# A masked softmax of a batched matmul: from scheduled tiles to hand-written engine programs with loops

## The chip, the cores and the metric

The kernel runs on one core of one Trainium2 chip. The metric is the device time of one execution in microseconds (us), lower is better. A core has five engines that run their own instruction streams: TensorE (PE in the profile; PEld is its weight load), VectorE (DVE), ScalarE (ACT), GpSimd (POOL) and SyncE (SP), and 16 DMA engines that move data. Most executions agree within some 0.3%, a few are over 1.5% longer.

## The reference

```python
# x: 16 x 512 x 512, weight: 512 x 512, scale = 0.125, mask = strict lower triangle, all f32
y = scale * np.matmul(x, weight)
y = np.where(mask == 1, y, -1e9)
y_exp = np.exp(y - np.max(y, axis=-1, keepdims=True))
out = y_exp / np.sum(y_exp, axis=-1, keepdims=True)      # f32
```

16.8 MB of x are read and 16.8 MB are written, with 1 MB of weights. Row r has r unmasked columns, so the upper half of each matrix needs only the first 256 columns.

## The kernel before

The work is cut into 16 units of 1 MiB. A *unit* takes, for two matrices of the batch, the upper (even unit) or lower (odd unit) 256 rows, laid on 128 partitions as 4 row groups. Two units are a *pair*. A unit goes through: load (SP queue), cast to bf16 (VectorE), 16 transposes (TensorE), their eviction from PSUM (where TensorE puts its results) half by VectorE and half by ScalarE, 16 products and 4 additions of the mask's band (TensorE), 4 exponentials with row sums (ScalarE), reciprocals and 4 scalings (VectorE), store (SP queue). Tiles come from pools, and the framework puts in the semaphores.

```python
def multiply(u):
    NC = (u % 2 + 1) * HB                                # 256 columns, or 512
    for t in range(T):
        py = psum_y.tile([P, N], FP32, name="py")
        for kt in range(KT):
            seq(nc.tensor.matmul(py[:, :NC], lhsT=xt[:, kt, t], rhs=w_bf[:, kt, :NC], ...))
        seq(nc.tensor.matmul(py[:, h * HB : NC], lhsT=ident_bf, rhs=band[:, h, t], ...))
        seq(nc.scalar.activation(out=ot[:, t, :NC], in_=py[:, :NC], func=AF.Exp, ...,
                                 accum_out=rsum[:, t : t + 1]))

def normalise(u):
    seq(nc.vector.reciprocal(rinv, st_sum.pop(u)))
    for t in range(T):
        seq(nc.vector.tensor_scalar_mul(ot[:, t, :NC], ot[:, t, :NC], rinv[:, t : t + 1]))
    ...
# [...] loads in the order x0, m0, weights, m1, x1, m2, x2, m3, x3 ... (m: a 64 KB block of the mask)
for u in range(U + 1):                                   # all written out, 16 units
    if u + 1 < U: transpose(u + 1)
    # [...] cast(u + 2), evict(u + 1)
    if u < U: multiply(u)
    if u >= 1:
        normalise(u - 1); store(u - 1)
        if u - 1 + X_BUFS < U: load(u - 1 + X_BUFS)
```

Loads and stores share the one SP queue; there are 8 load buffers and 8 store buffers.

The softmax here doesn't subtract the row's maximum and nothing guards it: scores larger than these inputs give would overflow.

## Time and profile before

| | before |
|---|---|
| time, median of 3 (range) | 90.67 us (90.64 to 90.68) |
| profiled execution: time, span | 90.53, 88.75 us |
| first load issued, first packet | 0.74, 2.18 us |
| last store issued | 80.01 us |
| its 16 parts landed: median, last | 86.19, 87.73 us |
| last instruction | 88.75 us |

The span runs from the first to the last instruction of the profiled execution; the rest of the measured time, 1.78 us, lies outside it. The page cuts the span in 40 slices of 2.2 us, where a 9 means busy for 90% or more. The prediction below shows the page's own lines. TensorE is full but stops 11 us before the end (at 77.3 us; VectorE at 80.0), and the DMA is full from slice 3 to the end. Each of the 37 transfers leaves 16 landing records (592 in all), one for the share of each DMA engine, and what follows waits for the last: the last store's come from 85.71 to 87.73 us and the last instruction at 88.75, so the end is that of the *slowest* of 16.

### The profile page before, as it was taken

To read this page: it belongs to the slowest core of one execution; us is meant where nothing else is said; L and a number is where in the kernel's file an instruction comes from. 1 tells how busy PE (TensorE), PEld (TensorE's weight loads), DVE (VectorE), ACT (ScalarE), POOL (GpSimd) and SP (SyncE) were. 2 spreads that over 40 slices of the span, in tenths; PEclk is the share of its full clock that TensorE was granted. 3 is DMA by queue.
4 is the path that set the end of the run, shared out by engine and by line. 5 is a ranking of instruction groups with operands and counts; after the bars stand their busy time and mean duration, and the time that the engine had idled before them with its cause. 6 is when DMAs were issued, how large, how long until landed. Compare 5 with 4: busy or idle time off the path is not lost.

```text
span 88.8 us, 1632 instructions
## 1 busy us (share of the span) xinstructions
PE 71.3 (80%) x596; PEld 49.3 (56%) x596; DVE 60.6 (68%) x124; ACT 55.2 (62%) x154; POOL 7.3 (8%) x20
## 2 busy tenths in 40 slices
PE   4984409999999999999999999999999999800000
PEld 1324109875795598479659857965895695300000
DVE  5866485479799779949986987976594998070000
ACT  5401461887797686969777787977778786710000
POOL 7620000002001000200010020002000202000000
PEclk9999655899999999999999999999999999997555
DMA  0899999999999999999999999999999999999970
GB/s 15 306 373 384 381 376 428 417 432 428 414 425 417 425 436 428 402 417 432 428 428 417 428 421 421 425 436 425 421 417 432 425 421 425 428 432 428 425 306 26
DMA packets 5334, 34.95 MB, mean 394 GB/s; under 512 B 592, under 2 KB 1104, under 8 KB 1104
## 3 DMA queue, kind: packets, MB, share of 16 engines
q1 hardware_dynamic: 5328, 34.87, 94.6%
q8 instruction: 4, 0.07, 0.3%
q14 instruction: 2, 0.02, 0.0%
HBM read 18.09 MB, written 16.78 MB: 393 GB/s over the span
## 4 chain that ended last, share of the span: by engine, by line
PE 72%; DMA 10%; DVE 3%; SPq 2%; ACT 1%; DVEq 0%; issue 0%; ACTq 0%
PE py L116 47%; PE pt L92 16%; DMA xf<-in_x_dram 10%; PE py L125 8%; DVE ot L152 1%; DVE xb L83 1%; SPq L163 1%; SPq L78 1%; ACT ot L135 1%; PE py L215 0%; SPq L167 0%; DVEq L284 0%; DVE rinv L150 0%; ACTq L284 0%
## 5 line engine op out<-in xcount | busy, mean ns | idle before, releaser
L116 PE MATMUL py<-w_bf,xt 128*128 128x256 bf16 (+1 forms) x256 | 50.0, 329 | 0.0
L135 ACT ACTIVATE ot<-py 128x256 f32<-128x256 f32 (+1 forms) x64 | 31.2, 493 | 7.5 <-PE py L125 7.1
L116 PEld LDWEIGHTS <-xt 128*128 128x128 bf16 x256 | 24.8, 99 | 12.2
L103 ACT COPY xt<-pt 128x1024 bf16<-128x1024 bf16 x16 | 16.2, 1012 | 12.9 <-PE pt L92 8.8
L152 DVE TENSOR_SCALAR ot<-ot,rinv 128x256 f32<-128x256 f32 (+1 forms) x64 | 23.5, 431 | 0.8
L83 DVE CAST xb<-xf 128x2048 bf16<-128x2048 f32 x16 | 19.5, 1220 | 5.0 <-DMA xf<-in_x_dram 5.0
L92 PE MATMUL pt<-ident_bf,xb 128*128 128x128 bf16 x256 | 17.8, 225 | 3.7 <-DVE xb L83 3.7
L92 PEld LDWEIGHTS <-xb 128*128 128x128 bf16 x256 | 16.6, 115 | 5.8 <-DVE xb L83 4.9
L125 PE MATMUL py<-band,ident_bf 128*128 128x256 bf16 x64 | 17.6, 275 | 0.0
L102 DVE COPY xt<-pt 128x1024 bf16<-128x1024 bf16 x16 | 11.0, 687 | 6.2 <-PE pt L92 6.2
L135 ACT ACTIVATION_READ_ACCUMULATOR ot<-py 128x1 f32 x64 | 12.8, 200 | 0.0
L154 POOL MEMSET ot<- 2x256 f32 x8 | 3.6, 448 | 65.7 <-DVE ot L152 65.7
L125 PEld LDWEIGHTS <-ident_bf 128*128 128x128 bf16 x64 | 6.3, 99 | 4.2
L180 PE MATMUL py<-zeros 128*128 128x512 bf16 x12 | 5.2, 619 | 1.2 <-DVE zeros L177 1.2
L150 DVE RECIPROCAL rinv<-rsum 128x4 f32<-128x4 f32 x16 | 2.7, 168 | 2.8 <-ACT ot L135 2.8
L186 DVE MEMSET ot<- 128x1024 f32 x4 | 3.6, 912 | 0.6 <-issue 0.6
L180 PEld LDWEIGHTS <-zeros 128*128 128x128 bf16 x12 | 1.6, 144 | 3.9 <-issue 2.8
L226 DVE CAST band<-py 64x256 bf16<-64x256 f32 x4 | 1.6, 414 | 2.5 <-PE py L215 2.5
L215 PE MATMUL py<-diag_bf,spread 128*128 128x256 bf16 x8 | 1.6, 339 | 1.2 <-DVE diag_bf L202 1.2
L226 ACT CAST band<-py 64x256 bf16<-64x256 f32 x4 | 1.4, 367 | 1.4 <-DVE band L226 1.4
L193 ACT ACT_TABLE_LOAD x1 | 1.3, 1283 | 0.7 <-PEq L270 0.7
L215 PEld LDWEIGHTS <-spread 128*128 128x128 bf16 x8 | 0.9, 111 | 1.5 <-issue 1.3
(14 smaller groups left out, 7.5 us busy)
## 6 DMA issues: line engine op xcount, KB each, us to landing
xf<-in_x_dram SPq DMA_DIRECT2D x16, 1024.0 KB, 13.7
out_dram<-ot SPq DMA_DIRECT2D x16, 1024.0 KB, 11.9
w_f<-in_weight_dram SPq DMA_DIRECT2D x1, 1024.0 KB, 7.0
diag_f<-in_mask_dram SPq DMA_DIRECT2D x4, 64.0 KB, 7.7
```

The costliest lines, as they stand in the source:

```text
L83: seq(nc.vector.tensor_copy(xb, st_x.pop(u)))
L92: nc.tensor.transpose(st_pt[u][kt // 2][:, kt % 2, t], xb[:, t].rearrange("p (k kt) -> p kt k", kt=KT)[:, kt], ident_bf,)
L102: seq(nc.vector.tensor_copy(xt[:, 0:2], pt[0]))
L103: seq(nc.scalar.copy(xt[:, 2:4], pt[1]))
L116: nc.tensor.matmul(py[:, :NC], lhsT=xt[:, kt, t], rhs=w_bf[:, kt, :NC], start=(kt == 0), stop=(kt == KT - 1),)
L125: nc.tensor.matmul(py[:, h * HB : NC], lhsT=ident_bf, rhs=band[:, h, t], start=False, stop=True, skip_group_check=True,)
L135: nc.scalar.activation(out=ot[:, t, :NC], in_=py[:, :NC], func=AF.Exp, bias=0.0, scale=float(scale), accum_out=rsum[:, t : t + 1],)
L152: seq(nc.vector.tensor_scalar_mul(ot[:, t, :NC], ot[:, t, :NC], rinv[:, t : t + 1]))
L154: seq(nc.gpsimd.memset(ot[0:2, 0, :HB], 1.0 / N))
L180: seq(nc.tensor.matmul(idle, lhsT=zeros[:, :P], rhs=zeros, start=True, stop=True))
L186: nc.vector.memset(ots[i][:, :, HB:], 0.0)
L226: seq(copy(band[half, h, t : t + 2, g * P : (g + 1) * P], src[half, :, g]))
```

## The change

Its intent is to take instruction fetches, waits and VectorE instructions away. Everything stands in one section with hand-made semaphores. TensorE's program is a loop over 8 pairs that starts on a 256-instruction edge, ScalarE's is a loop of two rounds over 4 pairs, and VectorE's is written out; both start on a 128-instruction edge. A pair does both transposes, then both products. One `tensor_tensor` with a broadcast operand normalises a unit. The second load and the second mask block go ahead of the weights.

```diff
-    const = ctx.enter_context(tc.tile_pool(name="const", bufs=1))
-    [...] all pools
+    section.enter_context(tc.tile_critical(no_gpsimd_drain=True))
+    [...] fixed buffers and 59 semaphores
     load(0)
     load_mask(0)
-    seq(nc.sync.dma_start(w_f32, weight...))
-    load_mask(1)
-    load(1)
+    load(1)
+    load_mask(1)
+    nc.sync.dma_start(w_f32, weight...).then_inc(s_w, 16)
     [...]
-        for t in range(T):
-            seq(nc.vector.tensor_scalar_mul(ot[:, t, :NC], ot[:, t, :NC], rinv[:, t : t + 1]))
+        nc.vector.tensor_tensor(
+            out=ot, in0=ot, in1=r.unsqueeze(2).to_broadcast([P, T, NC]), op=ALU.mult
+        ).then_inc(s_norm, 1)
     [...]
+    tensor.addr_align(BLOCK, max_nops=0)
+    [...]
+    with tensor.Fori(1, U // 2 + 1) as n:
+        for i in range(2):
+            tensor.wait_ge(s_cast[i], n)
+            transpose(i)
+        with tensor.If(n < 2):
+            spin(3)
+            [...] spread the mask into the band
+        multiply(0, n)
+        multiply(1, n)
+    section.close()
+    with tc.tile_critical(no_gpsimd_drain=True):
+        nc.sync.wait_ge(s_end, 16 * OUT_BUFS)
+        nc.sync.sem_clear(s_end)
```

## The prediction

> **What bounds the kernel now.** I read the page's busy slices first, then its DMA queues, then the waits of the sync engine's queue, then the groups by form, then windows over the last microseconds, and last the trace's single DMA packet and landing records.
>
> ```profile
> PE   4984409999999999999999999999999999800000
> DVE  5866485479799779949986987976594998070000
> DMA  0899999999999999999999999999999999999970
> GB/s 15 306 373 384 381 376 428 417 432 428 414 425 417 425 436 428 402 417 432 428 428 417 428 421 421 425 436 425 421 417 432 425 421 425 428 432 428 425 306 26
> q1 hardware_dynamic: 5328, 34.87, 94.6%
> q8 instruction: 4, 0.07, 0.3%
> q14 instruction: 2, 0.02, 0.0%
> ```
>
> TensorE is full from slice 8, but it and every other engine stop by slice 36; the DMA is full from slice 3 to slice 38. At the middle rate of about 425 GB/s, 34.87 MB take 82.0 us. The first packet starts at 2.2 us, the first 13 us run at 376 to 384 GB/s, and the last data lands near 87.7 us. So the transfers set the end, though the page's chain of work is 72% TensorE.
>
> ```profile
> SPq L158 <- DVE ot L152: 49.8, 15, 9.6
> SPq L284 <- DMA out_dram<-ot: 7.1, 2, 4.7
> ...
> 80.01 0.54 SPq L158 DMA_DIRECT2D out_dram<-ot  x1
> ...
> 84.50:85.00 0.50, 0.00 (x0) 0.00 (x0) 0.00 (x0) 0.00 (x0) 0.00 (x0) 0.50 0.97 410
> 85.00:85.50 0.50, 0.00 (x0) 0.00 (x0) 0.00 (x0) 0.00 (x0) 0.00 (x0) 0.50 0.97 410
> 85.50:86.00 0.50, 0.00 (x0) 0.00 (x0) 0.00 (x0) 0.00 (x0) 0.00 (x0) 0.50 0.51 213
> 86.00:86.50 0.50, 0.00 (x0) 0.00 (x0) 0.00 (x0) 0.00 (x0) 0.00 (x0) 0.50 0.35 147
> 86.50:87.00 0.50, 0.00 (x0) 0.00 (x0) 0.00 (x0) 0.00 (x0) 0.00 (x0) 0.50 0.31 131
> ```
>
> The last store is issued at 80.01 us and the end waits for stores alone. The windows (next to last column: mean busy share of the 16 DMA engines) show a ragged end: full to 85.5, then about a third of the engines busy for 1.5 us more. The landing records say which: the 16 parts of the last store land between 85.71 and 86.46 for ten engines, and between 87.14 and 87.73 for six. Parts of one load land within 0.5 us of each other until 20 us; from 23.8 us one straggles by 1.2 us, later two, four, six. The packet records name a cause: four packets of 16,384 bytes on queue 8 (instructions) start at 21.5, 35.5, 50.4 and 63.3 us and take 0.9 to 1.1 us; two of 8,192 bytes on queue 14 come at 35.9 and 39.2. Six fetches, six late engines.
>
> [...]a pair of units has 146 TensorE instructions in 7.86 us, so 256 take 13.8 us, against 13 to 15 us between the fetches. [...]each of 16 engines signals its own share and only all 16 mean landed; the landing records show just that, so the slowest engine sets the end. [...]No tensor_tensor is in this trace[...].
>
> **The change part by part.** The groups by form that I calculate with:
>
> ```profile
> L116 PE MATMUL py<-w_bf,xt 128*128 128x512 bf16 x128 | 31.6, 379 | 0.0
> L83 DVE CAST xb<-xf 128x2048 bf16<-128x2048 f32 x16 | 19.5, 1220 | 5.0 <-DMA xf<-in_x_dram 5.0
> L103 ACT COPY xt<-pt 128x1024 bf16<-128x1024 bf16 x16 | 16.2, 1012 | 12.9 <-PE pt L92 8.8 <-ACT ot L135 4.1
> L152 DVE TENSOR_SCALAR ot<-ot,rinv 128x512 f32<-128x512 f32 x32 | 13.4, 483 | 0.3
> L102 DVE COPY xt<-pt 128x1024 bf16<-128x1024 bf16 x16 | 11.0, 687 | 6.2 <-PE pt L92 6.2
> L152 DVE TENSOR_SCALAR ot<-ot,rinv 128x256 f32<-128x256 f32 x32 | 10.1, 379 | 0.5
> ```
>
> *Instruction fetches.* The changed TensorE program is about 190 instructions in a loop that starts on a 256-instruction edge, so none of the four 16 KiB fetches should fall into the busy part; the ScalarE and VectorE programs start on 128-instruction edges and hold fewer than 128, so the two 8 KiB ones go too. What stays is at the start, before data flows. The end moves from the slowest of the late engines, 87.73, to the slowest of the others, 86.46: -1.27 us. This is on the path.
>
> *Transfers.* The same 33 transfers of 1 MiB and four mask blocks, one queue, same order but for one load ahead of the weights. Loads 3 to 7 no longer wait for earlier landings (4.0 us of waits), but DMA was never short of work there: 0.
>
> *Edges.* The section adds a barrier after the first one and one more hop at the end: some +0.25 us before the first load is issued (an estimate from the 0.4 to 0.5 us that one complete barrier takes at the end of this trace). At the end one wait replaces four semaphore waits in a row (0.25 us), which pays for the extra hop: 0.
>
> *Normalising.* Per pair, 4 x 317 + 4 x 420 ns (start to start in the timeline) = 2.95 us become [...]1.22 + 2.29 = 3.51 us: VectorE gains 0.56 us of work per pair. Its pair is then two evictions 1.3, a gap of 0.3 between them, two reciprocals with a self-wait 0.5, 3.5, two casts 2.4: 8.0 us. In the middle this is hidden. At the end the last unit's 2.29 against 1.68 is exposed to the last store's issue.
>
> *Order on TensorE.* Before, unit u+1's transposes run ahead of unit u's products, and a pair takes 7.86 us with no idle. Now a pair is two transposes (1.78), then two products (2.19 + 3.89). The first product needs both halves of its eviction: ScalarE is free about 0.72 us after the last matmul of the pair before and copies for 1.01, so TensorE starts at 1.8 to 1.9 in place of 1.78. [...]Pair: 7.86 + 0.1 to 0.3 = 8.0 to 8.15.
>
> *First pair.* Its products now wait for both transposes, the whole mask and the weights. Tile 1 lands at about 9.1 (where the weights landed), cast to 11.0, transposes at half clock to 12.9 (they took 1.90 cold before), eviction and mask to 13.9, three spins and four spreads to 15.3, copies to 16.3: products at 16.4 against 15.0. But two units are then ready: the first pair ends near 22.8, against 23.2.
>
> *Sum for compute.* 22.8 + 7 x 8.0 to 8.15 = 78.8 to 79.9; last exponential 0.7, reciprocal 0.3, product 2.3: the last store is issued at 82.1 to 83.2 in place of 80.0. The first load took 1.44 us from issue to first packet, and the last store's first packet ran at 83.59, so the store is in time if issued by 82.15 + 0.25 = 82.4. Overrun: 0 to 0.8 us, say 0.3.
>
> *Total.* 90.67 - 1.27 + 0.25 + 0.3 = about 90.0.
>
> **The rivals.** *(a) Compute takes the bound over.* The slack of the last store, 2.1 us, is nearly all spent. Every 0.1 us on a pair is worth 0.7 us at the end: a pair of 8.4 us would give 92, and a loop-back that fetches (0.9 to 1.1 us per fetch here) would give 97. For it: VectorE's pair at 8.0 has no room left. Against: the edge alignment is there just for this. *(b) The fetches are not what makes engines late,* or another comes near the end (leaving the loop): then the end stays ragged, and the change only adds its edges: 90.9 to 91.5. *(c) All hidden and the early dips shrink too:* the mask blocks cost short dips (141 to 200 GB/s for 0.2 us each); two of them now stand next to each other, the gain is at most 0.3: 89.2.
>
> **Range and chances.** My path is 90.0; (c) and an absent overrun give 89.2; a pair of 8.25 us gives 91.3. So 89.1 to 91.5. Faster by over 2% means under 88.86, below the transfers' floor as I have it: 6%. Slower by over 2% means over 92.48, a pair of over 8.4 us: 8%. Within 2%: 86%.
>
> **What would show it.** Right: no packet of 16,384 bytes on queue 8 between 3 and 80 us; the last store's 16 landings within 0.8 us; DMA share falling from 1.0 to 0 in half a microsecond; same GB/s in the middle; VectorE's product at 1.2 and 2.3 us; pair period 8.0 to 8.15; last store issued at 82 to 83. Wrong: fetches or long idle of TensorE at the loop's branch, a DMA share under 0.9 before the last store (compute is the bound), stragglers without fetches (rival b), or a first load issued later than 1.2 us.

The sum came to 90.67 - 1.27 + 0.25 + 0.3 = 89.95, "about 90.0". The 1.22 and 2.29 us of the products came from the cut rule, for no `tensor_tensor` had been measured; VectorE's pair of 8.0 us and, through the last store at 82.1 to 83.2, the overrun of 0.3 use them. That a loop on an edge has no fetches was an estimate: the 16 KB fetches of before start 12.9 to 14.9 us apart, and at 146 TensorE instructions in 7.86 us that is 239 to 278 of them, some 256 to a fetch and half as many to one of 8 KB.

## The result

| us | before | after |
|---|---|---|
| median of all runs | 90.68 (4 runs) | 91.56 (91.33 to 93.88, 4 runs) |
| ratio of fast runs, 95% interval | | 1.0084 (1.0064 to 1.0104) |

A ratio is the mean time of one kernel's fast runs over that of the other's fast runs of the same rounds, so it is not quite the ratio of the medians. The change made the kernel 0.8% slower: the same within 2%, but clearly not the hoped-for gain, and just above the range that was given.

The profiled run of that measurement fell in the slow state (93.88 us), so the unaltered kernel was run again. All four runs of it were fast (91.48 to 91.63, ratio 1.0099), and its profile, of a run of 91.48 us, is "after" from here on. This is its page: the busy slices of two engines, the clock that TensorE was granted, the DMA, and the DMA queues with their packets, MB and share.

```profile
span 89.4 us, 1673 instructions
...
PE   0995179699999999999999999999999999950000
DVE  2865727966089979997998899799889979719000
PEclk9999855699999999999999999999999999998555
DMA  0799999999999999999999999999999999999860
GB/s 15 286 348 351 393 370 425 429 425 425 433 425 418 422 433 425 425 425 433 422 425 429 425 429 433 425 422 425 433 422 425 433 429 418 425 436 418 359 271 7
q1 hardware_dynamic: 5328, 34.87, 93.9%
q8 instruction: 1, 0.02, 0.1%
q14 instruction: 2, 0.02, 0.1%
```

The bytes and the middle rate (some 425 GB/s) are those of before. The fetches have gone: queue 8 has one packet in place of four, and the packet records put the start of all three that are left between 1.9 and 2.2 us, before the first data packet at 2.46 (the 16 KB one lasts to 3.3). Yet the last slice of the DMA is as thin as before. The windows of the last microseconds show why (each line: the window, its length, busy time of the five engines, the clock, the mean share of the 16 DMA engines, GB/s):

```profile
86.00:86.50 0.50, 0.00 (x0) 0.00 (x0) 0.00 (x0) 0.00 (x0) 0.00 (x0) 0.50 0.68 279
86.50:87.00 0.50, 0.00 (x0) 0.00 (x0) 0.00 (x0) 0.00 (x0) 0.00 (x0) 0.50 0.08 33
87.00:87.50 0.50, 0.00 (x0) 0.00 (x0) 0.00 (x0) 0.00 (x0) 0.00 (x0) 0.50 0.04 16
87.50:88.00 0.50, 0.00 (x0) 0.00 (x0) 0.00 (x0) 0.00 (x0) 0.00 (x0) 0.50 0.04 16
88.00:88.50 0.50, 0.00 (x0) 0.00 (x0) 0.00 (x0) 0.00 (x0) 0.00 (x0) 0.50 0.00 0
```

Before, a third of the engines worked on for 1.5 us. Now the share drops to 0.04, and one engine of 16 is a share of 0.06: a *single* engine holds the end. The landing records of the last store say the same:

```
last store's parts landed (us)   median   last six                               last instruction
before                           86.19    87.14 87.18 87.22 87.52 87.65 87.73    88.75
after                            86.86    86.88 86.89 86.90 86.91 86.93 88.38    89.38
```

Six late engines have become one, and the one is as late against the median (1.52 us) as the latest of the six was (1.53). The lag of the last part behind the median, transfer by transfer, shows how it got there:

```
after: median landing   27.6   47.2   57.0   66.8   76.6   83.9   86.9
lag of the last part    0.48   0.48   0.83   1.22   1.80   2.01   1.52
lag of the next to last 0.31   0.45   0.45   0.45   0.45   0.50   0.07
```

No fetch happens in that time, but one engine drifts: it loses 1.5 us between 47 and 84 us and the second-latest loses nothing. The last store lets the others wait a little (their engines idle for about half a microsecond in front of it, for it was issued late), so 0.5 us of the lag is hidden again.

Where the time went, from the two profiled runs:

| us | before | after | difference |
|---|---|---|---|
| first load issued | 0.74 | 0.97 | +0.23 |
| moved by 15 us (packets under way counted in part) | 4.717 MB | 4.521 MB | |
| last store issued | 80.01 | 82.71 | +2.70 |
| last store landed, median engine | 86.19 | 86.86 | +0.67 |
| last store landed, last engine | 87.73 | 88.38 | +0.65 |
| last instruction after that | 1.02 | 1.00 | -0.02 |
| outside the span | 1.78 | 2.10 | +0.32 |
| sum | 90.53 | 91.48 | +0.95 |

0.20 MB fewer by 15 us are 0.46 us at 425 GB/s; 0.23 of it is the later first load. The first two issues of the sync engine, the after kernel's first and then the one of before (start, length, line):

```profile
0.97 0.67 SPq L121 DMA_DIRECT2D xf<-in_x_dram  x1
```

```profile
0.74 0.67 SPq L78 DMA_DIRECT2D xf<-in_x_dram  x1
```

The compute side did what was expected of it. Two groups by form of the after kernel, with count, busy time and mean ns:

```profile
L206 DVE TENSOR_TENSOR ot<-ot,rinv 128x2048 f32<-128x2048 f32 x8 | 18.3, 2292 | 0.3
L206 DVE TENSOR_TENSOR ot<-ot,rinv 128x1024 f32<-128x1024 f32 x8 | 9.8, 1224 | 0.3
```

From its timeline, two evictions of VectorE that stand one pair apart, and the sync engine's last store (start, length; in brackets the idle time before and what ended it):

```profile
40.55 0.69 DVE L197 COPY xt<-pt 128x1024 bf16<-128x1024 bf16 x1 [0.35 <-PE pt L302]
...
48.51 0.69 DVE L197 COPY xt<-pt 128x1024 bf16<-128x1024 bf16 x1 [0.35 <-PE pt L302]
...
82.71 0.54 SPq L140 DMA_DIRECT2D out_dram<-ot  x1
```

One instruction of 2.29 us replaces four of 483 ns, one of 1.22 replaces four of 379; the pair takes 48.51 - 40.55 = 7.96 us; the last store goes out at 82.71.

### The profile page after: what moved, and what is told of

The parts are those of the page before. It is cut to its first block, busy times and chain, and to the rows that moved or that the text cites. A ratio compares the mean times of both kernels' runs of the same rounds, so it can differ in the third digit from the quotient of the medians.

```text
span 91.8 us, 1665 instructions
## 1 busy us (share of the span) xinstructions
PE 74.4 (81%) x587; PEld 49.8 (54%) x595; DVE 65.8 (72%) x76; ACT 56.6 (62%) x154; POOL 6.2 (7%) x20
## 4 chain that ended last, share of the span: by engine, by line
PE 73%; DMA 7%; DVE 6%; SPq 3%; issue 2%; ACT 0%; ACTq 0%; DVEq 0%
PE py L317 47%; PE pt L302 16%; PE py L324 8%; DMA diag_f<-in_mask_dram 7%; DVE ot L206 2%; SPq L121 2%; DVE band L228 2%; PE py L336 1%; DVE xb L193 1%; SPq L125 1%; PE py L351 0%; DVE diag_bf L214 0%; ACT ot L285 0%; DVE rinv L204 0%; ACTq L267 0%
## 5 line engine op out<-in xcount | busy, mean ns | idle before, releaser
L317 PE MATMUL py<-w_bf,xt 128*128 128x256 bf16 (+1 forms) x248 | 49.3, 331 | 1.3 <-DVE band L228 0.8
L285 ACT ACTIVATE ot<-py 128x256 f32<-128x256 f32 (+1 forms) x64 | 31.4, 491 | 14.9 <-PE py L324 13.7
L317 PEld LDWEIGHTS py<-w_bf,xt 128*128 128x128 bf16 x256 | 25.1, 100 | 15.1 <-issue 1.7
L206 DVE TENSOR_TENSOR ot<-ot,rinv 128x1024 f32<-128x1024 f32 (+1 forms) x16 | 28.1, 1759 | 0.5
L302 PE MATMUL pt<-ident_bf,xb 128*128 128x128 bf16 x256 | 16.6, 225 | 3.7 <-DVE xb L193 3.7
L302 PEld LDWEIGHTS pt<-ident_bf,xb 128*128 128x128 bf16 x256 | 15.8, 115 | 5.6 <-DVE xb L193 4.7
L324 PEld LDWEIGHTS py<-band,ident_bf 128*128 128x128 bf16 x64 | 6.4, 100 | 4.3
L336 PE MATMUL py<-zeros 128*128 128x512 bf16 x15 | 6.8, 631 | 2.0 <-DVE zeros L231 2.0
L178 POOL MEMSET ot<- 2x256 f32 x8 | 2.4, 304 | 71.1 <-DVE ot L206 71.1
L336 PEld LDWEIGHTS py<-zeros 128*128 128x128 bf16 x15 | 2.1, 145 | 5.0 <-issue 5.0
L351 PE MATMUL py<-diag_bf,spread 128*128 128x512 bf16 x4 | 1.9, 633 | 0.0
```

The lines of the kernel that those rows point to most:

```text
L206: nc.vector.tensor_tensor(out=ot, in0=ot, in1=r.unsqueeze(2).to_broadcast([P, T, NC]), op=ALU.mult).then_inc(s_norm, 1)
L285: nc.scalar.activation(out=ots[b][:, t, :NC], in_=pys[t][:, :NC], func=AF.Exp, bias=0.0, scale=float(scale), accum_out=rsums[b][:, t : t + 1],
L302: last = tensor.transpose(pts[i][kt // 2][:, kt % 2, t], xb[:, t].rearrange("p (k kt) -> p kt k", kt=KT)[:, kt], ident_bf,)
L317: tensor.matmul(pys[t][:, :NC], lhsT=xts[h][:, kt, t], rhs=w_bf[:, kt, :NC], start=(kt == 0), stop=(kt == KT - 1),)
L324: tensor.matmul(pys[t][:, h * HB : NC], lhsT=ident_bf, rhs=band[:, h, t], start=False, stop=True, skip_group_check=True,).then_inc(s_py[h] ...
L336: tensor.matmul(pys[0], lhsT=zeros[:, :P], rhs=zeros, start=True, stop=True)
```

## The experiments

Four theories of the loss were on the table. *A, compute:* the later last store (normalising, a longer pair, the cold first pair) sets the end. *B, the slow engine:* one DMA engine drifts for another reason than the fetches and sets the end, so their removal gains nothing. *D, the start:* the new load order costs early bandwidth. *The edges:* what stands before the first load, after the last landing and outside the span. The expectations use these letters, and three more: *C* is B made precise (one engine loses about 2 us of its own between 28 and 80 us, in every kernel), *E* is the edges, and *F*, added last, is a reason for the drift. All runs gave right results. The ranges given for e_raw1, e_raw_best and e_flat hold one or two slow executions each, which the ratios leave out. The trace of e_order is of an execution of 93.72 us and that of e_raw_best of one of 91.40, 1.0 and 0.5 us above their medians.

**The unaltered kernel again** gave the profile above.

> The changed kernel once more, unaltered, for a profile in the fast state (the first one fell in the slow state, at 93.88 us). Theory A, compute has become the bound: about 91.5 us, pairs of 7.96 us on TensorE from 25.4 us on, last store issued at 84.5 to 84.7 us, and several DMA engines idle for about 1 us right before the last store's packets. Theory B, the transfers still bound it because some engines are delayed by fetches at the start or by something else: the engines' shares of the last store stay back to back with the store before, with no idle before them, and the landings are ragged by 1 us or more.

The median was 91.56, ratio 1.0099 (1.0082 to 1.0116). Fifteen engines had idle time before the last store and the sixteenth had nearly none: that is B's picture, not A's.

**A warm TensorE.** The granted clock is halved during the first pair (5 and 6 in slices 6 to 8; 0.50 from 11 to 16 us). With more idle matmuls it stayed up (in the page below; its mean is 0.967 in place of 0.921).

```diff
-WARM = 12
+WARM = 16
             transpose(i)
+            if i == 0:
+                with tensor.If(n < 2):
+                    spin(10)
```

> Four more idle matmuls at the start and ten between the first and the second unit's transposes, so that TensorE's clock does not fall before the first pair. Theory A: second transposes take 1.0 us in place of 1.9, spreads and first products run at full clock, the first pair ends near 22.5 us in place of 25.4, all later pairs come 2.5 to 3 us earlier, and the time falls to the transfers' floor, 89.3 to 90.0 us. Theory B: the pairs come earlier just the same, but the time changes by less than 0.3 us.

The page's clock row, the last store in the sync engine's timeline, and two windows of the end:

```profile
PEclk9999999999999999999999999999999999999655
```

```profile
81.38 0.54 SPq L140 DMA_DIRECT2D out_dram<-ot  x1
```

```profile
86.00:86.50 0.50, 0.00 (x0) 0.00 (x0) 0.00 (x0) 0.00 (x0) 0.00 (x0) 0.50 0.09 33
...
87.50:88.00 0.50, 0.00 (x0) 0.00 (x0) 0.00 (x0) 0.00 (x0) 0.00 (x0) 0.50 0.00 0
```

The clock is full and the last store goes out 1.33 us earlier (81.38 against 82.71). The fifteen engines end about 0.47 us earlier (median 86.39), the sixteenth only 0.18 (88.20). The time: 91.43, ratio 1.0086 (1.0069 to 1.0103). 1.33 us of compute bought 0.13 us, which is within the noise. A falls.

**Normalising of the last unit as before**, by four `tensor_scalar`.

```diff
+        if u == U - 1:
+            for t in range(T):
+                last = nc.vector.tensor_scalar_mul(ot[:, t], ot[:, t], r[:, t : t + 1])
+            last.then_inc(s_norm, 1)
+            return
```

> Only the last unit is normalised by four scalar products of 0.42 us (start to start) in place of one tensor product of 2.29 us; nothing else. Theory A: last store issued 0.6 us earlier, time lower by 0.5 to 0.6 us, about 90.9 us. Theory B: within 0.15 us of the changed kernel.

The last store went out at 82.04, 0.67 us earlier, and the time did not follow: 91.64, ratio 1.0117 (1.0084 to 1.015), last landing 88.64. A falls here too.

**No alignment.**

```diff
-    nc.vector.addr_align(BLOCK // 2, max_nops=0)
-    nc.scalar.addr_align(BLOCK // 2, max_nops=0)
-    tensor.addr_align(BLOCK, max_nops=0)
```

> The changed kernel without the three instructions that start the programs of TensorE, VectorE and ScalarE at a block's edge. If the edges matter, TensorE's loop now straddles one and fetches in the loop: instruction packets of 16,384 bytes in most pairs, 1 us or more of TensorE idle at each, 95 us or more. If loops fetch nothing[...], no packets after 25 us and the time within 0.3 us of the changed kernel, perhaps lower because the fetches at 2 us are gone.

91.45, ratio 1.0083 (1.0066 to 1.01). The three early fetches vanish, two of 8 KB come at 37.6 and 53.9 us, none of 16 KB at all, and TensorE shows no stall at the loop's branch (busy 54.22 of the 55 us from 25 to 80, against 54.42 with the alignment). The last landing was 88.62. The alignment buys nothing here: this loop of some 190 instructions ran its eight rounds without a 16 KB fetch where it happened to start. Why, no run shows.

**The fetches put back.** TensorE's loop was written out on top of the warm kernel. It is the direct test of the prediction's first term.

```diff
-    with tensor.Fori(1, U // 2 + 1) as n:
+    for n in range(1, U // 2 + 1):
 [...] e_warm's edit, and plain tests of n inside
```

> The kernel with the warm clock, TensorE's program written out in place of its loop, so that its instruction fetches fall into the transfers again. Theory C: one DMA engine loses about 2 us of its own between 28 and 80 us (packets of 320 to 360 ns in place of 309, all in one chain) in every kernel, and is last in all of them; fetches on other engines are then hidden: four packets of 16,384 bytes, time within 0.4 us of the 91.43 us of the looped one. My prediction's theory, fetches are on the path: 1.0 to 1.3 us slower, 92.5 us.

The page's instruction queue, and the windows of the end:

```profile
q8 instruction: 5, 0.08, 0.3%
```

```profile
86.50:87.00 0.50, 0.00 (x0) 0.00 (x0) 0.00 (x0) 0.00 (x0) 0.00 (x0) 0.50 0.27 115
87.00:87.50 0.50, 0.00 (x0) 0.00 (x0) 0.00 (x0) 0.00 (x0) 0.00 (x0) 0.50 0.31 131
87.50:88.00 0.50, 0.00 (x0) 0.00 (x0) 0.00 (x0) 0.00 (x0) 0.00 (x0) 0.50 0.12 49
```

```
last store's parts landed (us)   median   last six
e_warm (loop)                    86.39    86.47 86.51 86.55 86.60 86.84 88.20
e_warm_unroll (written out)      86.58    86.97 87.92 88.07 88.19 88.31 88.43
```

Four fetches of 16 KB come back (28.8, 39.6, 53.2, 68.8 us, 0.93 to 1.01 us each), and with them four more late engines and the third of a share in the windows. The time stays: 91.43, ratio 1.0084, against 91.43 and 1.0086 with the loop (other rounds, on another chip). So a fetch does make an engine late, as the prediction said, and that is hidden behind an engine that is late anyway, as it did not. How late, the packet records show: the fetch takes its 0.93 to 1.01 us, the data packet that starts as it ends takes 0.70 to 0.85 in place of 0.31, so some 1.3 to 1.5 us in all, and the five late engines land 1.34 to 1.85 us behind the median. In the kernel before, the four fetches took 0.89 to 1.10 us and the data packet behind each 0.77 to 0.86, some 1.43 to 1.56 us in all (0.63 and 0.95 with the two of 8 KB), and the engine stays late: the lag of the last part was 1.52 us at 22 us, after the first fetch, and 1.46 at 35.

**Less work for one engine.** If one engine is slow, a store that spares it should let it catch up. The store of unit 10 was split into 120 and 8 rows, in three kernels: on the warm one, on its written-out form and on the kernel before. I supposed that this spares the slow engine one store's share, 2.45 us (the measured time from store to store), if it is the last-numbered; no run shows which engine a row goes to, nor the slow engine's number.

```diff
+        if u in SPLIT:                                   # SPLIT = (10,)
+            nc.sync.dma_start(dst[:60], src[:120]).then_inc(done, 16)
+            nc.sync.dma_start(dst[60:], src[120:]).then_inc(done, 16)
+        [...] else as before; the final wait counts one transfer more
```

> The kernel with the warm clock; the store of unit 10 is issued as 120 rows and 8 rows[...]. Theory C, with the slow engine the last-numbered one: it ends 0.6 us before the others, [...]last landing near 87.0 in place of 88.2 us, time 90.2 to 90.6 us. If the slow engine is another, or the lag is not an engine's own: 91.4 to 92.0 us.

> Both: the store split and TensorE's program written out. Theory C: with the slow engine spared, the engines that fetches delay become the last, so the loop now shows its worth: 0.4 to 1.2 us slower than the split kernel with the loop, 90.8 to 91.5 us. If fetches never matter: within 0.3 us of it.

> The kernel before, with the store of unit 10 split in the same way and nothing else. Theory C: the slow engine is spared, but four to five engines delayed by instruction fetches lag almost as far (1.3 to 1.45 against 1.5 us), so it gains only 0.1 to 0.4 us: 90.3 to 90.6 us. If the slow engine is not the last-numbered: 90.7 to 91.3 us.

| | median us | ratio | last landing |
|---|---|---|---|
| e_warm_split | 93.98 | 1.0364 (1.0347 to 1.0382) | 90.94 |
| e_warm_split_unroll | 92.92 | 1.0238 (1.0205 to 1.027) | 89.92 |
| b_split | 92.26 | 1.0214 (1.0157 to 1.0271) | 89.40 |

All three lost, because the split store itself was slow: between 71 and 77 us packets took up to 1062, 1336 and 845 ns where 309 is usual. Why, no run shows. The test of B failed, and these runs decide nothing: whether the latest engine of the first of them (90.94) was the one meant to be spared is not shown either.

**The load order of before.**

```diff
-    load(1)
-    load_mask(1)
     nc.sync.dma_start(w_f32, ...).then_inc(s_w, 16)
+    load_mask(1)
+    load(1)
 [...] likewise load(2) goes ahead of load_mask(3)
```

> The changed kernel with the loads in the order of the kernel before (weights third, a mask block after each large load) and nothing else. The DMA moved 4.72 MB by 15 us in the kernel before and 4.45 to 4.53 in the hand-written ones, 0.45 to 0.63 us of transfer; the later first load explains 0.23 of it. Theory D, the rest is lost where two mask blocks come one after the other: 4.60 MB or more by 15 us and 0.2 to 0.3 us faster, 91.3 us. Rival, fetches at 2.1 us or nothing to do with order: under 0.1 us.

The last store in the sync engine's timeline, and two windows around it:

```profile
84.67 0.54 SPq L141 DMA_DIRECT2D out_dram<-ot  x1
```

```profile
84.50:85.00 0.50, 0.00 (x0) 0.00 (x0) 0.14 (x1) 0.00 (x0) 0.00 (x0) 0.50 0.47 197
85.00:85.50 0.50, 0.00 (x0) 0.00 (x0) 0.00 (x0) 0.00 (x0) 0.00 (x0) 0.50 0.17 66
```

92.74 (92.35 to 93.72), ratio 1.0229 (1.0189 to 1.027): "unclear" against 2%, yet above the changed kernel. 4.55 MB had moved by 15 us, hardly more than 4.52, so here D falls. (Another pair says a little else: e_raw_best below had 4.66 MB by 15 us and e_raw_na_warm, which differs from it in the load order alone, 4.57. D may be worth up to 0.2 us.) What changed is the second tile: cast at 12.42 us in place of 10.47. The last store went out at 84.67 and the DMA had to wait for it (share 0.17): here compute *is* the bound, and all 16 engines land late (median 88.81). With both transposes ahead of both products the second tile is needed early, so its place ahead of the weights belongs to the change. It also shows how little room compute has: 2 us more, in this execution, and it takes over.

**No section, no framework context.** The kernel's programs were given to the bare instruction builder, and the wait for the last stores went to the end of SP's own program.

```diff
-    with _tile.TileContext(nc) as tc:
-        tile_matmul_scale_mask_softmax_kernel(tc, *args)
+    class _Raw:
+        def __init__(self, nc):
+            self.nc = nc
+        def tile_critical(self, **_):
+            return ExitStack()                           # a section that does nothing
+    tile_matmul_scale_mask_softmax_kernel(_Raw(nc), *args)
 [...]
     nc.sync.sem_inc(s_issued, 1)
+    nc.sync.wait_ge(s_end, 16 * OUT_BUFS)
+    nc.sync.sem_clear(s_end)
 [...]
-    with tc.tile_critical(no_gpsimd_drain=True):
-        nc.sync.wait_ge(s_end, 16 * OUT_BUFS)
-        nc.sync.sem_clear(s_end)
```

> The same five programs without the two sections around them: no barrier and no extra jump after the launch's own barrier, the wait for the last stores at the end of the sync engine's program. Theory E, the changed kernel's loss lies at its edges (0.23 us before the first load, some 0.3 us outside the span that the before kernel does not have): first load issued near 0.75 us, time less span back to 1.8 us, 0.5 to 0.9 us faster, 90.7 to 91.0 us. Rival, the edges only move work about and one slow DMA engine sets the end anyway: under 0.2 us.

Beside it ran e_raw_best, which has this edit and those of e_order, e_warm and e_noalign:

> No sections, loads in the order of before, warm clock, no alignment of the programs. If D and E both hold: 1.0 us or more faster than the changed kernel, 90.2 to 90.6 us, faster than both. If only E: as e_raw1.

And e_flat, which keeps the sections, drops the alignment and writes both loops out:

```diff
-    with nc.scalar.Fori(1, U // OUT_BUFS + 1) as n:
+    for n in range(1, U // OUT_BUFS + 1):
 [...]
-    with tensor.Fori(1, U // 2 + 1) as n:
+    for n in range(1, U // 2 + 1):
 [...] no alignment, the warm-up and the tests of n written out
```

> The changed kernel with both loops written out and no alignment: hand-written programs and one product per unit stay. If the loops or the alignment cost or save anything: more than 0.3 us from 91.5 us. I expect none of it: 91.3 to 91.7 us, time less span still 2.1 us, with instruction packets of 16,384 bytes back in the middle.

The first gave 90.07 (89.46 to 91.5), ratio 0.9908 (0.987 to 0.9947): faster than both kernels, on a chip whose times scattered. The second gave 90.91, ratio 1.0001: the load order took the gain back, with the last store at 83.84 and all engines late. The third gave 92.04 (91.36 to 92.89), ratio 1.0087 (1.0063 to 1.0111). Its four 16 KB fetches were back and its span was 89.03, none the longer: the loops save nothing in the span. But three of its six executions (92.46 to 92.89) had 3.3 to 3.5 us outside the span, against 2.0 to 2.1 in the others (91.36 to 91.63), and the ratio fits the latter alone. The profiled run is one of the long ones (92.55, 3.52 us outside), with one more 16 KB fetch after the span, at 91.3; e_warm_unroll, with TensorE's loop alone written out, never showed this.

On another chip e_raw1 was repeated unaltered, then with e_warm's edit (e_raw_warm), then with that and e_noalign's (e_raw_na_warm):

> The kernel without the sections once more, because its six times on the last chip ran from 89.46 to 91.50 us. If the edges are what the change lost: 0.4 to 1.0 us faster than the kernel before, 89.7 to 90.3 us, in fast runs of this chip too. If the last result was that chip's noise: 90.7 us or more.

> Without the sections, with the warm clock. The pairs come about 1.5 us earlier, but the one slow engine sets the end: within 0.3 us of the kernel without the sections. If compute was the bound after all once the edges are gone: 0.5 us faster or more.

> As the last, without the alignment of the three programs. If the fetches that the alignment puts at 2.1 us delay the first loads by about 0.3 us for good: 0.2 to 0.4 us faster than the last. If, as between the changed kernel and the one without alignment, nothing comes of it: within 0.15 us.

| | median us (range) | ratio to before (95%) |
|---|---|---|
| before, same rounds | 90.58 (90.49 to 90.74) | |
| e_raw1_again | 89.56 (89.41 to 89.88) | 0.9891 (0.9871 to 0.9911) |
| e_raw_warm | 89.46 (89.37 to 89.51) | 0.9872 (0.9857 to 0.9887) |
| e_raw_na_warm | 89.51 (89.48 to 89.56) | 0.9883 (0.9868 to 0.9898) |

The first load and the last store in e_raw_warm's timeline:

```profile
0.75 0.66 SPq L121 DMA_DIRECT2D xf<-in_x_dram  x1
...
81.09 0.54 SPq L140 DMA_DIRECT2D out_dram<-ot  x1
```

Of the waits of its sync engine (line, what it waited for; us in all, times, longest) the one for the last stores, after which the program ends:

```profile
SPq L147 <- DMA out_dram<-ot: 6.5, 1, 6.5
```

In the changed kernel's same view the wait for the stores is followed by waits of the closing section and context, for other engines:

```profile
SPq L361 <- DMA out_dram<-ot: 4.2, 1, 4.2
SPq L381 <- PEq L381: 0.7, 1, 0.7
SPq L395 <- PEq L395: 0.5, 2, 0.4
```

Without the edges the first load is back at 0.75 us, the last instruction comes 0.05 us after the last landing in place of 1.00, and 1.33 us lie outside the span in place of 2.10. Set against the changed kernel's profile that is 0.22 + 0.95 + 0.77 = 1.94 us, which is about the whole difference between the profiled runs (91.48 - 89.56 = 1.92). The last landing, 88.19 and 88.14 us, is still that of one engine, and later than before's 87.73. e_raw_warm beats both kernels: 1.3% under before in its rounds. Against the changed kernel no run shares its rounds; the ratios to before (0.9872 and 1.0099) put it at about 2.2% under.

**What slows the one engine? (F)** The slow packets of the drift are parts of stores that take 320 to some 370 ns in place of 309, most of them one after the other in one chain. They go with the engines' work: in the kernel before the last comes at 77.4 us, though stores run on to 87. F says: records or signals that come with each instruction pass by that engine. 60 semaphore increments on GpSimd after each of the 8 memsets, 480 in all, are to add such traffic and no work (the trace has 2145 instructions in place of 1673).

```diff
         nc.gpsimd.memset(ots[u % OUT_BUFS][0:2, 0, :HB], 1.0 / N).then_inc(s_row, 1)
         nc.gpsimd.wait_ge(s_row, u // 2 + 1)
+        for _ in range(60):
+            nc.gpsimd.sem_inc(s_tick, 1)
```

> The changed kernel with 480 more semaphore increments on GpSimd, 60 after each of its eight memsets, to no purpose; GpSimd is idle there. What slows one engine's store packets is not known; theory F, it is the writing of the profile's own record of each instruction, since its slow packets come only in stores and only while instructions run: some 29% more records, so 0.3 to 0.8 us more of lag on that one engine and a time of 91.8 to 92.3 us. If it is something else: lag and time as in the changed kernel, 91.4 to 91.7 us.

```
e_ticks: median landing 27.7   47.3   57.1   66.9   76.7   84.0   87.0
lag of the last part    0.84   1.08   1.30   1.84   2.65   3.0    2.50
```

The last eight stores count on one semaphore and follow each other every 2.45 us. From 74 us on the lag is so long that the landings of two stores overlap, and records cut into sixteens by time alone would show a lag that stops at 2.2. The values at 76.7 and 84.0 us were found by following the slow packets from store to store; the second is good to some 0.1 us.

92.24, ratio 1.0181 (1.0166 to 1.0197). The last store went out at 82.79, as in the changed kernel; the last landing came at 89.49 in place of 88.38, while the median engine ended at 86.98 in place of 86.86. So the run confirms that the latest of 16 engines sets the time. Of the 0.98 us of additional lag some 0.4 was there by 20 us, before the first increments (behind the memset at 22.0). The rest is a faster drift: from 27.7 to 76.7 us the lag grows by 1.81 us, against 1.32 in the changed kernel. The packets say the same without the landings. Between 68 and 78 us, when only stores run and no fetch falls in this run, the store packets of 320 to 399 ns lose 0.76 us in all over 309 ns each; in each of the other kernels that leave the stores whole, *the kernel before among them*, they lose 0.46 to 0.53 us.

That speaks for F, whose forecast of the time (91.8 to 92.3 us) came true: 28% more instruction records (2145 in place of 1673) went with half as much drift again. It is one run, though, with four new 8 KB instruction fetches (28.6, 47.5, 64.0, 80.1 us), and it does not part the records, which the profiler writes, from the signals. What in the increments slows the engine stays open.

## Why the prediction was right or wrong

**Wrong: "Instruction fetches", -1.27 us, "This is on the path".** This is the step that failed. The fetches went, and the latest of their engines with them, but the end did not move to "the slowest of the others, 86.46". The last landing came at 88.38, 0.65 us later than before, on an engine that no fetch in the busy part had touched. I counted six fetches and six late engines and took the one for the cause of the other. The count was a coincidence. Followed from transfer to transfer, five of the six jump back at a fetch (the four of 16 KB and the 8 KB one at 35.9 us); the engine of the other 8 KB fetch lost some 0.6 us and seems not to be among them. The sixth drifts: between the fetches at 50.4 and 63.3 us one lag grows from 0.55 to 0.88 us while the others stay. It is the drift of the changed kernel, of the same pace (0.50 us lost in slow packets between 68 and 78 us, in both), hidden in the crowd. The written-out loop shows both halves: fetches bring back four late engines, and the time stays. Rival (b), "The fetches are not what makes engines late", is half right in its reason, half wrong (they do, but others are late as well), and right in its result: its 90.9 to 91.5 is the nearest of the four.

**Partly right: "Transfers", 0.** The steady rate is the same. But 0.46 us are lost by 15 us, of which the later first load explains 0.23. The rest is not explained: it is there without the sections too (4.53 to 4.57 MB in those kernels, with the first load at 0.75) and with the load order of before (4.55); with both it was smaller (4.66).

**"Edges", +0.25 and 0.** The start measured +0.23: right. At the end, from the last landing to the last instruction, 1.02 became 1.00: right. Missed was what lies outside the span, +0.32 us, for which no view of the kernel before had a line. It goes, and more, when the sections go, so it belongs to them or to the context around them.

**"Normalising": right.** Expected 1.22 and 2.29 us, measured 1.22 and 2.29 (1224 and 2292 ns).

**"Order on TensorE", 8.0 to 8.15: right in kind, 0.04 too high at its lower end.** Measured 7.96. Measured, TensorE was busy 10.00 us in each 10 us from 20 to 70, so the loop's branches cost it no idle time.

**"First pair": right in kind, too early.** The products were expected at 16.4 and began at 17.5 us. Still the **last store**, expected at 82.1 to 83.2, went out at 82.71.

**Smaller slips.** The parts of one load land within 0.5 to 0.74 us of each other until 20 us, not within 0.5; and by the prediction's own sums a pair of 8.25 us gives 91.1, not 91.3.

**"Overrun", 0.3: wrong reasoning, small loss.** It took the last store's issue to be on the path. It delayed fifteen engines by about half a microsecond, but the end is the sixteenth's: 1.33 us of earlier issue gave 0.13.

**Sum.** The prediction's sum was -1.27 + 0.25 + 0.3 = -0.72. The two profiled runs give, term by term: fetches 0, as they were hidden; first load +0.23; the rest of the last landing's delay +0.42; tail -0.02; outside the span +0.32: together +0.95, of which the medians show 0.85 to 0.88. The range ended at 91.5; with rival (b) weighed higher it would have held 91.56. "Within 2%" was right.

**Open:** what about the instructions slows the one engine (F has one run for it), the second half of the early loss, and what exactly the 0.32 us outside the span are.

## What to carry to other kernels

When a transfer ends only with the slowest of 16 engines, taking away one cause of lateness gains nothing until you know how late the *next* one is (here six late engines became one, 1.52 us behind the median in place of 1.53); look for a late engine in a stretch without the cause before calling a saving "on the path". When transfers share a semaphore, do not cut their landing records into groups by time alone: a late part then hides in the next transfer (in e_ticks a lag of 3.0 us showed as 2.2). Here, where data movement was the bound, half a microsecond at each edge was worth more than compute in the middle: 1.33 us of earlier issue bought 0.13 us (e_warm), and all the gain was in leaving out the closing and opening of the sections (1.9 us). TensorE's loop took the 16 KB fetches out of the busy part (none from 3 us on; four with it written out, e_warm_unroll) and the alignment two of 8 KB (e_noalign has them, at 37.6 and 53.9 us), and both were worth nothing measurable in the span; only with all loops and alignment gone (e_flat) did half of the executions lose 1.3 to 1.4 us outside it.
